# Encoder layer on one core: the Fourier branch on sums and differences of mirrored tokens, channels and weight rows, with three gate blocks ahead of the attention

## The chip, the cores and the metric

The kernel runs on one core of one Trainium2 chip. The metric is the device time of one execution in microseconds (us). Five engines work beside each other, each through its own queue of instructions: PE (TensorE) multiplies matrices, and its weight loads are shown apart as PEld; DVE (VectorE) and ACT (ScalarE) do elementwise work; POOL (GpSimd) does a little; SP (SyncE) starts the transfers from HBM. Instructions wait for each other through semaphores.

## The reference

One layer of a bidirectional encoder on 256 tokens of 2048 channels, in float32:

```python
def _macaron_ffn(x, pre_g, w_gate, w_up, w_down, post_g):
    return x + MACARON_WEIGHT * _rms_norm(_swiglu(_rms_norm(x, pre_g), w_gate, w_up, w_down), post_g)
...
def _fourier_mix(f):
    b, s = f.shape[0], f.shape[1]
    fg = f.astype(jnp.float32).reshape(b, s, FOURIER_GROUPS, FOURIER_GROUP_DIM)
    mixed = jnp.real(jnp.fft.fft2(fg, axes=(1, 3), norm='ortho'))
    return mixed.reshape(b, s, FOURIER_WIDTH).astype(f.dtype)
...
    u = _rms_norm(h, pre_g)
    q, k, v, f, g = jnp.split(u @ w_in, SPLIT_POINTS, axis=-1)
    q = _apply_axial_rope(_rms_norm(q.reshape(b, s, N_Q_HEADS, HEAD_DIM), q_norm_g), rope)
    k = _apply_axial_rope(_rms_norm(k.reshape(b, s, N_KV_HEADS, HEAD_DIM), k_norm_g), rope)
    v = v.reshape(b, s, N_KV_HEADS, HEAD_DIM)
    y_attn = _blocked_gqa(q, k, v) @ w_attn_o
    y_four = _fourier_mix(f) @ w_fourier
    gates = jax.nn.sigmoid((g.reshape(b, s, N_BRANCHES, D_MODEL) + b_gate).astype(jnp.float32)).astype(h.dtype)
    merged = gates[:, :, 0] * y_attn + gates[:, :, 1] * y_four
    return h + _rms_norm(merged @ w_out, post_g)
```

The layer is a first feed-forward half-step (width 5632), the gated mixers above, and a second feed-forward half-step. `w_in` has 2048 columns of q, 512 of k, 512 of v, 1024 of f (8 groups of 128 channels) and twice 2048 of gates; there are 16 query heads on 4 key heads.

## The kernel before

**Products.** Every float32 product is made of three matmuls in the fp32r format (`mm3`, L97 to L100): both factors are split into a rounded part (`hi`) and what is left (`lo`), and hi*hi, hi*lo and lo*hi are summed in PSUM. `split` (L92 to L95) does this with one copy on ACT (L93) and one subtraction on DVE (L94). A weight piece is two k-tiles of 128 x 512; `piece` loads it into a buffer `raw` (five of them) and splits it into `whi` and `wlo` (six pairs). So DVE and ACT can be at most six pieces ahead of PE.

**Blocks.** `col_block` (L179) multiplies the normalised tokens `u` (two token tiles of 128) with 512 columns of a weight: 16 k-tiles, two token tiles, three matmuls each, 96 matmuls of 512 columns. `between` spreads other work over such a block. `row_block` (L209) multiplies a chunk of 512 channels with 512 rows of a weight, again 96 matmuls, and DVE adds the result to `y`.

**The mixers' order.** v (with the norms of the first half-step's end), q of the first four heads, the two blocks of f (L556); then four rounds j, one for each key head: the gate block of the Fourier branch (`gate(12 + j)`, with the Fourier transforms in the first of them), the scores of four heads (`attn_scores`, L609), the Fourier branch's output columns (`four_cb`, L677), the next q block with the products with v between its matmuls (`attn_parts`), and the attention's output rows. The gates of the attention branch (blocks 8 to 11 of `w_in`) come in and after the last round, with `merged` (L711) and the rows of `w_out` between them.

**The Fourier branch.** f is computed for 256 tokens and 1024 channels with 192 matmuls of 512 columns (`fch`). For each group of 128 channels `fourier_positions` (L566) multiplies with the cosines and sines of the positions (six matmuls of 258 columns), and `fourier_channels` (L578) with those of the channels (six matmuls of 130 and 128 columns); the sines of position 256 - k are those of k negated, so only positions 0 to 128 are computed. `four_cb` multiplies the result with `w_fo`: 192 matmuls of 512 columns over the four rounds.

**Scores.** `attn_scores` makes four score tiles `sc` of two heads each, in a ring of three PSUM tiles. For each, DVE takes the maximum (`mx`, L619) and negates it (`nmx`), ACT takes the exponential of both halves (L624), and DVE forms `rinv` and scales `p` (L629). The fourth tile needs the room of the first. ACT loads a table of functions before the gate's sigmoid (L673) and another before the exponential.

**What sets the order.** The code is written in one order, and a scheduler puts the instructions of each engine into one fixed sequence when the kernel is built. On the chip each engine goes through its sequence in that order: an instruction that waits holds up everything behind it on its engine.

Of the kernel before, what the change touches and what calls it, by code (L numbers as in the profile page):

```python
# [18 lines left out]
P = 128  # L19
D = 2048  # L20
# [10 lines left out]
GROUPS = 8  # L31
EPS = 1e-6
# [14 lines left out]
def encoder_layer(  # L47
# [4 lines left out]
    mix_pre, w_in, b_gate, q_g, k_g, w_ao, w_fo, w_out, mix_post,  # L52
    f2_pre, f2_gate, f2_up, f2_down, f2_post,
    rope_cos, rope_sin, dft_pos, dft_ch, ident_in,
# [49 lines left out]
    def piece(src, k0, n, pools=None):  # L104
        """k-tiles k0 .. k0 + n of a chunk of weights: raw, hi, lo."""
# [73 lines left out]
    def col_block(u, w, nb, between=()):  # L179
        """u @ w[nb] for both token tiles: PSUM tiles. between: pieces of other work, spread over the block."""  # L180
# [3 lines left out]
        for kg in range(KD // CK):  # L184
            wt = weights(w[nb, kg])
            for k in range(CK):
                kk = kg * CK + k
                if done < len(between) and kk >= (done + 1) * step:
# [8 lines left out]
    def row_part(ch, wt, t, cb, y, first=False, part=slice(0, NB)):  # L197
# [5 lines left out]
        if first:  # L203
            V.tensor_copy(dst, ps)
# [4 lines left out]
    def row_block(ch, w, rb, y, first, between=()):  # L209
        """y += ch @ w[rb]; between[cb] comes ahead of column block cb."""  # L210
# [7 lines left out]

    def last_rows(ch, w, rb, y, norm, nxt=None, w_next=None):
        """The last row block, token tile 0 first, and the norms behind it; then the first column block of what  # L220
        follows, its token tile 0 while token tile 1 gets ready. VectorE's order is given: it has the most to do here."""
# [97 lines left out]
    class PostNorm:  # L319
        """h += half * rms_norm(y) * g_post per token tile."""  # L320
# [40 lines left out]
    class NextInput:  # L361
        """u = transpose(h * g_pre), rs[t] = rsqrt(mean(h^2)); y is room."""
# [32 lines left out]
    def ffn(u, rs, wg, wu, wd, y, tail, gate0, w_next=None, early=()):  # L395
        """tail() loads what the end needs and gives what to do with y."""
# [36 lines left out]
    zero = const.tile([P, NB], BF16, name="zero")  # L433
# [44 lines left out]
    # column blocks of w_in: 0-3 q, 4 k, 5 v, 6-7 f, 8-11 gate A, 12-15 gate B  # L478
# [4 lines left out]
    gq = const.tile([P, HD], F32, name="gq")  # L483
    gk = const.tile([P, HD], F32, name="gk")
    load(gq[:], q_g.partition_broadcast(P))
    load(gk[:], k_g.partition_broadcast(P))
    rc = const.tile([P, NT, HD], F32, name="rc")
    rsn = const.tile([P, NT, HD], F32, name="rsn")
# [14 lines left out]
    def norm_rope(ps, nm, t):  # L503
        """r * ps, RMS norm of each head, gain and rotation."""
# [3 lines left out]
        junk = work("junk")  # L508
        A.activation(q[:], ps[t][:], AF.Copy, scale=rs[t][:, 0:1])
        for j in range(4):  # L510
            A.activation(junk[:, j * HD:(j + 1) * HD], q[:, j * HD:(j + 1) * HD], AF.Square,
                         accum_out=ssq[:, j:j + 1])
        r = rsqrt(ssq[:], 4, 1.0 / HD, "rh")
        q3 = q[:].rearrange("p (j c) -> p j c", j=4)
        V.tensor_tensor(out=q3, in0=q3, in1=r[:].unsqueeze(2).to_broadcast([P, 4, HD]), op=ALU.mult)
# [13 lines left out]
    pv = col_block(u, w_in, 5, between=[nxt.finish])  # L529
    kro = [norm_rope(pk, "k", t) for t in range(NT)]  # L530
    vs = big("vs", F32R, [P, 2, NT, NB])
    for t in range(NT):
# [282 lines left out]
```

## Time and profile before

| | |
|---|---|
| median of 3 runs | 2108.99 us (2108.08 to 2109.59) |
| span of the profiled execution | 2107.7 us |
| ACT busy | 971.3 us (46%) |
| weight splits on DVE (L94, x727) | 887.3 us, 1221 ns each |
| weight splits on ACT (L93, x727) | 769.1 us, 1059 ns each |
| chain that ended last | PE 96%, DVE 3%, DMA 1% |
| moved by DMA | 406.23 MB, 193 GB/s on average |

The chain that ended last is the work followed back from the last instruction, at each step to what released it. It lies almost all on PE, so in this kernel time is first of all matmul time; the other engines' work counts where PE must wait for it. A matmul's duration in the profile (390 ns for 512 columns) runs until its last result is out, and the next one starts before that; what a matmul costs is the distance between starts.

### The profile page before, as it was taken

How to read it: one execution, taken by the hardware profiler on the slowest of the kernel's cores; microseconds unless marked ns; L12 is line 12 of the kernel's file. 1: busy time of each engine (PE TensorE's matmuls, PEld its weight loads, DVE VectorE, ACT ScalarE, POOL GpSimd, SP SyncE). 2: the span in 40 equal slices, each digit the busy share in tenths (PEclk: the TensorE clock that was granted, in tenths of full speed). 3: DMA queues.
4: the chain of work that ended last, by engine and by line, in shares of the span. 5: the costliest groups of instructions: out<-in, count | busy, mean ns of one | idle time of the engine just before them, and what ended most of it. 6: DMA issues, size and time to landing. Idle time of an engine off the chain costs nothing.

```text
span 2107.7 us, 25198 instructions
## 1 busy us (share of the span) xinstructions
PE 2089.4 (99%) x9528; PEld 1729.8 (82%) x9528; DVE 1290.4 (61%) x1660; ACT 971.3 (46%) x1232; POOL 33.3 (2%) x30
## 2 busy tenths in 40 slices
PE   9999999999999999999999999999999999999998
PEld 7888888888888878888888888778888888888886
DVE  6655555555555786676767666875555555555556
ACT  7444444444444555555455444554444444444443
POOL 0000000000000100000000000200000000000001
PEclk9999999999999999999999999999999999999999
DMA  8665655665656566455545556556566556665563
GB/s 313 229 216 190 190 191 189 196 189 188 193 191 192 178 216 202 145 195 200 180 156 184 191 194 194 194 196 209 193 189 191 189 192 195 189 190 187 194 192 108
DMA packets 112874, 406.23 MB, mean 193 GB/s; under 512 B 12528, under 2 KB 14320, under 8 KB 111344
## 3 DMA queue, kind: packets, MB, share of 16 engines
q1 hardware_dynamic: 112752, 404.61, 59.1%
q8 instruction: 75, 1.23, 0.2%
q14 instruction: 47, 0.39, 0.1%
HBM read 400.37 MB, written 4.19 MB: 192 GB/s over the span
## 4 chain that ended last, share of the span: by engine, by line
PE 96%; DVE 3%; DMA 1%; issue 0%; ACT 0%; SPq 0%; DVEq 0%; ACTq 0%
PE pc L100 20%; PE pc L99 20%; PE pc L98 20%; PE pr L98 10%; PE pr L100 10%; PE pr L99 10%; PE pt L169 2%; PE pf L98 1%; PE pf L100 1%; PE pf L99 1%; DVE wlo L94 1%; DVE h L356 0%; PE pt L640 0%; DMA raw<-in_f_gate 0%; DVE y L206 0%
## 5 line engine op out<-in xcount | busy, mean ns | idle before, releaser
L94 DVE TENSOR_TENSOR wlo<-raw,whi 128x1024 fp32r<-128x1024 f32 (+1 forms) x727 | 887.3, 1221 | 741.9 <-ACT whi L93 741.6
L93 ACT ACTIVATE whi<-raw 128x1024 fp32r<-128x1024 f32 (+1 forms) x727 | 769.1, 1059 | 1009.7 <-PE pc L100 606.7
L98 PE MATMUL pc<-whi,uh 128*128 128x512 f32 x1904 | 744.2, 391 | 1.8 <-ACT uh L451 1.8
L100 PE MATMUL pc<-whi,ul 128*128 128x512 f32 x1904 | 741.6, 390 | 2.3 <-DVE ul L94 2.3
L99 PE MATMUL pc<-wlo,uh 128*128 128x512 f32 x1904 | 741.6, 390 | 2.2 <-DVE wlo L94 2.2
L100 PEld LDWEIGHTS pc<-whi,ul 128*128 128x128 f32 x1904 | 357.4, 188 | 77.6 <-DVE ul L94 3.2
L99 PEld LDWEIGHTS pc<-wlo,uh 128*128 128x128 f32 x1904 | 357.5, 188 | 76.7 <-DVE wlo L94 4.2
L98 PEld LDWEIGHTS pc<-whi,uh 128*128 128x128 f32 x1904 | 357.5, 188 | 76.0 <-ACT uh L451 3.4
L98 PE MATMUL pr<-whi,hTh 128*128 128x512 f32 x688 | 269.5, 392 | 0.0
L100 PE MATMUL pr<-whi,hTl 128*128 128x512 f32 x688 | 268.0, 389 | 0.0
L99 PE MATMUL pr<-wlo,hTh 128*128 128x512 f32 x688 | 267.7, 389 | 0.0
L100 PEld LDWEIGHTS pr<-whi,hTl 128*128 128x128 f32 x688 | 129.1, 188 | 27.0
L99 PEld LDWEIGHTS pr<-wlo,hTh 128*128 128x128 f32 x688 | 129.2, 188 | 26.2
L98 PEld LDWEIGHTS pr<-whi,hTh 128*128 128x128 f32 x688 | 129.2, 188 | 26.1
L206 DVE TENSOR_TENSOR yf<-pr,yf 128x512 f32<-128x512 f32 (+1 forms) x82 | 55.1, 672 | 10.4 <-PE pr L100 9.7
L206 DVE TENSOR_TENSOR y<-pr,y 128x512 f32<-128x512 f32 x80 | 54.7, 685 | 4.1 <-PE pr L100 3.6
L98 PE MATMUL pr<-whi,oTh 128*128 128x512 f32 x128 | 49.8, 389 | 0.0
L99 PE MATMUL pr<-wlo,oTh 128*128 128x512 f32 x128 | 49.8, 389 | 0.0
L100 PE MATMUL pr<-whi,oTl 128*128 128x512 f32 x128 | 49.8, 389 | 0.0
L98 PE MATMUL pr<-whi,mTh 128*128 128x512 f32 x120 | 46.9, 391 | 0.0
L100 PE MATMUL pr<-whi,mTl 128*128 128x512 f32 x120 | 46.7, 389 | 0.0
L99 PE MATMUL pr<-wlo,mTh 128*128 128x512 f32 x120 | 46.7, 389 | 0.0
(218 smaller groups left out, 1188.2 us busy)
## 6 DMA issues: line engine op xcount, KB each, us to landing
raw<-in_f_up SPq DMA_DIRECT2D x176, 512.0 KB, 4.7
raw<-in_f_down SPq DMA_DIRECT2D x176, 512.0 KB, 4.6
raw<-in_f_gate SPq DMA_DIRECT2D x175, 512.0 KB, 4.6
raw<-in_w_in SPq DMA_DIRECT2D x128, 512.0 KB, 4.4
raw<-in_w_ao SPq DMA_DIRECT2D x32, 512.0 KB, 3.9
raw<-in_w_out SPq DMA_DIRECT2D x32, 512.0 KB, 4.5
raw<-in_w_fo SPq DMA_DIRECT2D x16, 512.0 KB, 4.7
h<-in_x SPq DMA_DIRECT2D x2, 1024.0 KB, 8.6
```

The source lines that it names most:

```text
L93: a = A.activation(hi, src, AF.Copy)
L94: v = V.tensor_tensor(out=lo, in0=src, in1=hi.bitcast(F32), op=ALU.subtract)
L98: T.matmul(ps, lh, rh, start=first, stop=False)
L99: T.matmul(ps, lh, rl, start=False, stop=False)
L100: return T.matmul(ps, ll, rh, start=False, stop=last)
L169: T.transpose(pt[:, j, :], src[:, j * P:(j + 1) * P], ident[:])
L206: V.tensor_tensor(out=dst, in0=ps, in1=dst, op=ALU.add)
```

## The change

Mirrored items (position p and 256 - p, channel c and 128 - c, and the rows of `w_fourier` likewise) have equal cosines and opposite sines, so the transform can run on sums and differences, each half as large.

- **Token order.** On the host the tokens are put in mirrored order (`_mirror`), so that token tile 1 is the mirror of tile 0, and the result is put back. `fold_tokens` makes sum and difference of the two tiles of the normalised tokens on DVE and transposes them (`ueo`): 32 transposes in all, in the v block and the first gate block.
- **f.** `fold_f` takes a piece of f's weight (16 pieces), makes sums and differences of mirrored channels on DVE (`dif`, and in place in `raw`), splits both, and multiplies the 260 sum columns with the token sums and the 252 difference columns with the token differences: 12 matmuls a piece, 192 in all. The tokens 0 and 128, which are no mirrored pair, are put right with a running sum `zs` on DVE, two steps a piece. The pieces are woven into the first q block (5), gate block 11 (6) and gate block 12 (5) by the new argument `at` of `col_block`.
- **Transforms.** `fourier_positions` and `fourier_channels` have 42 and 44 small matmuls, of 126 to 130 columns, in place of 48 of 258 and 48 of 128 to 130.
- **Output.** `fourier_out(cb)` takes the place of `four_cb`: for each of four pieces of `w_fo` DVE makes the sum `s` and the difference (in place in `raw`) of mirrored weight rows, both are split, and 6 matmuls follow; channel 64 of each group and token 128 are added by three further matmuls (`mids`, and `first` with `dh` and `dl`, the split of a running sum `acc` kept on DVE). That is 27 matmuls of 512 columns in each round, in place of 48. Sum and difference of the two PSUM tiles then give the two token tiles (`w`), and these are multiplied with the gates.
- **Order.** The gates of the Fourier branch (blocks 10 to 13) now come ahead of the rounds and are kept in `mB`; the attention's gates take their place in the rounds. The merge and the rows of `w_out` follow the last round without gate blocks between them; the first two row blocks of `w_out` are summed in PSUM (`row_blocks`).
- **Moved from DVE to ACT.** The scaling of `p`, the scaling in `norm_rope`, and the first copy of each row result.

```diff
+    def fold_f(b, k0):
...
+        dif = work("dif", [P, WP, OW])
+        V.tensor_tensor(out=dif[:].rearrange("p k (g c) -> p k g c", g=GH), in0=pc, in1=qc, op=ALU.subtract)
+        V.tensor_tensor(out=pc, in0=pc, in1=qc, op=ALU.add)
...
+        split(hi[:, :, 0:EW], lo[:, :, 0:EW], raw[:, :, 0:EW])
+        split(hi[:, :, EW:NB], lo[:, :, EW:NB], dif[:])
+        for j in range(WP):
...
+            mm = mm3(pfold[b][:, e], ueo[0][0][:, k, :], ueo[0][1][:, k, :], hi[:, j, e], lo[:, j, e], k == 0, False)
+            with tc.issue_after(mm.ins):
+                mm3(pfold[b][:, o], ueo[1][0][:, k, :], ueo[1][1][:, k, :], hi[:, j, o], lo[:, j, o], False, k == KD - 1)
...
+                V.scalar_tensor_tensor(out=zs[b], in0=raw[:, j, 0:EW], scalar=o0[:, k:k + 1], in1=zs[b],
+                                       op0=ALU.mult, op1=ALU.add)
...
-                V.tensor_scalar(out=p[:, i, :], in0=p[:, i, :], scalar1=rinv[:, i:i + 1], scalar2=None, op0=ALU.mult)
+                A.activation(p[:, i, :], p[:, i, :], AF.Copy, scale=rinv[:, i:i + 1])
...
-    def four_cb(cb, gz):
+    def fourier_out(cb):
...
+        for j in range(4):
...
+            V.tensor_tensor(out=s[:], in0=raw[:, 0, :], in1=raw[:, 1, :], op=ALU.add)
+            V.tensor_tensor(out=raw[:, 1, :], in0=raw[:, 0, :], in1=raw[:, 1, :], op=ALU.subtract)
...
+            split(hi[:, 0, :], lo[:, 0, :], s[:])
+            split(hi[:, 1, :], lo[:, 1, :], raw[:, 1, :])
+            mm3(pe[:], foT[0][0][:, j, P:2 * P], foT[0][1][:, j, P:2 * P], hi[:, 0, :], lo[:, 0, :], j == 0, False)
+            mm3(po[:], foT[0][0][:, j, 0:P], foT[0][1][:, j, 0:P], hi[:, 1, :], lo[:, 1, :], j == 0, False)
...
+                V.scalar_tensor_tensor(out=acc[:], in0=s[:], scalar=dcol[:, j:j + 1], in1=acc[:], op0=ALU.mult, op1=ALU.add)
...
+        T.matmul(pe[:], mids[:], wn[0:NYR, :], start=False, stop=True)
+        dh, dl = workr("dh"), workr("dl")
+        split(dh[:], dl[:], acc[:])
+        T.matmul(po[:], first[:], dh[:], start=False, stop=False)
+        T.matmul(po[:], first[:], dl[:], start=False, stop=True)
...
+        for t, op in ((0, ALU.add), (1, ALU.subtract)):
+            w = work("w")
+            V.tensor_tensor(out=w[:], in0=pe[:], in1=os_[:], op=op)
+            V.tensor_tensor(out=cbs(mB[t], cb), in0=w[:], in1=cbs(mB[t], cb), op=ALU.mult)
+    gate(10, mB, 0, between=[lambda b=b: fold_tokens(b) for b in range(1, 4)]
+         + [lambda t=t: kro.append(norm_rope(pk, "k", t)) for t in range(NT)])
+    pq = col_block(u, w_in, 0, at=folds_at(5))
+    qs = []
+    gate(11, mB, 1, at=folds_at(6), between=[lambda t=t: qs.append(norm_rope(pq, "q", t)) for t in range(NT)])
+    gate(12, mB, 2, at=folds_at(5), between=[lambda t=t: turn_k(t) for t in range(NT)])
+    qT = new_chunk("qT")
+    gate(13, mB, 3, between=fourier_parts() + [lambda t=t: turn_q(qT, qs, t) for t in range(NT)])
...
     for j in range(4):
...
+            gate(5 + j, zA, j - 1, between=[lambda t=t: turn_q(qT, qs, t) for t in range(NT)])
         for t in range(NT):
             attn_scores(j, qT, t, ps)
-        four_cb(j, gz)
+        fourier_out(j)
```

Where the instructions now stand is shown at two places.

**The scores of a round, on DVE.** Before, in the first round, from the second gate tile on (`z` is the gate, `wlo` a split of weights for `four_cb` and the block behind it):

```order
L672 SCALAR_TENSOR_TENSOR z<-pc,r1r,bg 128x512
L619 TENSOR_REDUCE mx<-sc 128x2
L94 TENSOR_TENSOR wlo<-raw,whi 128x1024
L620 TENSOR_SCALAR nmx<-mx 128x2
L627 RECIPROCAL rinv<-rsum 128x2
L619 TENSOR_REDUCE mx<-sc 128x2
L629 TENSOR_SCALAR p<-p,rinv 128x256 x2
L620 TENSOR_SCALAR nmx<-mx 128x2
L94 TENSOR_TENSOR wlo<-raw,whi 128x1024
```

The same place in the change, from the third `rinv` of the first round on (`s` and `raw` are sum and difference of the first piece of `w_fo`):

```order
L732 RECIPROCAL rinv<-rsum 128x2
L724 TENSOR_REDUCE mx<-sc 128x2
L725 TENSOR_SCALAR nmx<-mx 128x2
L790 TENSOR_TENSOR s<-raw 128x512
L732 RECIPROCAL rinv<-rsum 128x2
L785 TENSOR_TENSOR wn<-nraw,wn 8x512
L791 TENSOR_TENSOR raw<-raw 128x512
L100 TENSOR_TENSOR wlo<-s,whi 128x512
L799 TENSOR_SCALAR acc<-s,dcol 128x512
L100 TENSOR_TENSOR wlo<-raw,whi 128x512
```

Before, the weights that PE needs behind the scores are split before the scores or between them; now the first of `w_fo` is touched behind the fourth maximum, and its split behind the fourth `rinv`. This is so in all four rounds.

**The same place on PE.** Before, the fourth score tile stands 17 matmuls of `four_cb` (`pf`) behind the third; these are the rows from the end of the third tile on, and the fourth begins at the next `sc` row:

```order
L100 MATMUL sc<-kT,qTl 128x256
L98 MATMUL pf<-whi,foTh 128x512
L99 MATMUL pf<-wlo,foTh 128x512
L100 MATMUL pf<-whi,foTl 128x512
L98 MATMUL pf<-whi,foTh 128x512
L99 MATMUL pf<-wlo,foTh 128x512
```

In the change the four score tiles stand together, and these rows, which begin with the last piece of `w_fo`, are the end of `fourier_out` (`pc` is the next q block):

```order
L104 MATMUL pf<-whi,foTh 128x512
L104 MATMUL pc<-whi,uh_5545 128x512
L104 MATMUL pc<-whi,uh_5695 128x512
L105 MATMUL pf<-wlo,foTh 128x512
L106 MATMUL pf<-whi,foTl 128x512
L104 MATMUL pf<-whi,foTh 128x512
L804 MATMUL pf<-wn,mids 128x512
L105 MATMUL pf<-wlo,foTh 128x512
L106 MATMUL pf<-whi,foTl 128x512
L807 MATMUL pf<-dh,first 128x512
L105 MATMUL pc<-wlo,uh_5545 128x512
```

Of the next block five matmuls stand ahead of the last one of `fourier_out` (`first` with `dl`), and all others behind it.

**The folds, on DVE.** A fold of f in the first q block of the change, which no row of before answers to (`wlo<-raw,whi 128x1024` is a whole weight piece of the block):

```order
L615 TENSOR_TENSOR dif<-raw 128x504
L630 SCALAR_TENSOR_TENSOR zs<-raw,o_5824,zs 128x260
L616 TENSOR_TENSOR raw<-raw 128x2x4x63
L100 TENSOR_TENSOR wlo<-dif,whi 128x2x252
L630 SCALAR_TENSOR_TENSOR zs<-raw,o_5824,zs 128x260
L100 TENSOR_TENSOR wlo<-raw,whi 128x2x260
L630 SCALAR_TENSOR_TENSOR zs<-raw,o_5824,zs 128x260
L100 TENSOR_TENSOR wlo<-raw,whi 128x1024 x2
```

A piece of f had one row of 128x1024 on DVE before; a fold has six.

More of the change, by code (lines that the diff above doesn't have):

```diff
@@ L592, in fourier_parts, with constant @@
-    def fourier_parts():
-        held = []
-        def part(n):
-            if n < 8:
-                new = fourier_positions(*divmod(n, 4))
-            if n > 0:
-                fourier_channels(*divmod(n - 1, 4), held.pop())
-            if n < 8:
-                held.append(new)
-        return [lambda n=n: part(n) for n in range(9)]
+    def constant(src, n):
+        raw = work("draw", [P, n])
+        load(raw[:], src)
+        return raw
+    WE, WO = P + 2, P
+    dps = const.tile([P, 2, WE + WO], F32R, name="dps")
@@ new lines, in _constants @@
+    odd = np.zeros((P, P + 2))
+    odd[:, 1:P:2] = 1.0
+    first = np.zeros((P, P))
+    first[:, 0] = 1.0
+    sign = 1.0 - 2.0 * (c % 2)
+    alt = np.zeros((P, GROUPS // 2, NYR))
+    mid = np.zeros((GH, 2 * P + 2 * NYR))
+    for g in range(GROUPS):
+        for at in (0, 32, 64):
+            alt[(g % 2) * HW:(g % 2 + 1) * HW, g // 2, at + g] = sign
+            mid[g % GH, 2 * P + (g // GH) * NYR + at + g] = 1.0
+        if g < GH:
+            mid[g, g * HW:(g + 1) * HW] = sign
+    ones = np.concatenate([odd, first, alt.reshape(P, -1)], 1)
```

354 lines of the change are left out of this document (236 added, 118 removed).

## The prediction

> **What bounds the kernel now.** I read the page's first part, then what PE waited for, then one round of the attention in a table of stretches, then the timeline of its scores.
>
> ```profile
> span 2107.7 us, 25198 instructions
> PE 2089.4 (99%) x9528; PEld 1729.8 (82%) x9528; DVE 1290.4 (61%) x1660; ACT 971.3 (46%) x1232; POOL 33.3 (2%) x30
> ```
> ```profile
> PE pc L100 <- DVE ul L94: 2.3, 2, 1.2
> PE pc L99 <- DVE wlo L94: 2.2, 3, 1.0
> ```
> ```profile
> core 0: us, PE busy (x) PEld busy (x) DVE busy (x) ACT busy (x) POOL busy (x), PEclk, DMA share, GB/s
> 887.80:972.80 85.00, 85.00 (x409) 71.06 (x408) 58.70 (x99) 45.00 (x74) 0.00 (x0) 1.00 0.59 201
> ```
>
> PE is busy for 99% of the span; its largest wait group is 2.3 us. In a round (from its first score matmul to the next round's) PE is busy for all 85 us, at full clock (1.00), and DVE for 58.7. So every matmul taken away shortens the time, as long as PE stays fed; DVE has 26.3 us to spare in a round, though not at every place. The question is where the change spends them.
>
> **The matmuls: 38.5 us less.**
>
> ```profile
> 499.65 0.39 PE L99 MATMUL pr<-wlo,hTh 128*128 128x512 f32 x1
> ...
> 505.77 0.39 PE L99 MATMUL pr<-wlo,hTh 128*128 128x512 f32 x1
> ```
> ```profile
> 856.36 0.28 PE L98 MATMUL pa<-dps,fh 128*128 128x258 f32 x1
> ...
> 857.08 0.40 PE L98 MATMUL pc<-whi,uh 128*128 128x512 f32 x1
> ```
> ```profile
> 862.19 0.22 PE L98 MATMUL pb<-ah,dcs 128*128 128x130 f32 x1
> ...
> 862.81 0.45 PE L98 MATMUL pc<-whi,uh 128*128 128x512 f32 x1
> ```
> ```profile
> 905.88 0.60 PE L640 MATMUL pt<-ident,p 128*128 128x128 f32 x4
> 906.24 0.48 PE L98 MATMUL pc<-whi,uh 128*128 128x512 f32 x1
> ```
>
> Starts give the cost: 27 steps from 499.65 to 505.77 are 0.227 us for 512 columns; six of 258 columns take 0.72 (0.12 each); six of 130 and 128 take 0.62 (0.103 each: these no longer shrink with their columns); four transposes 0.36. Removed: 384 of 512 columns (f and `four_cb`) 87.1, eight times 0.72 and eight times 0.62, together 97.8 us. Added: 192 of 252 or 260 columns at 0.12, 23.0; 86 small ones at 0.103, 8.9; eight fours of transposes, 2.9; 108 of 512, 24.5; together 59.3. The difference is **38.5 us**. Small ones with few stationary columns are not in the trace; between nothing and 0.103 for some twenty of them this is at most 2 us.
>
> **What DVE must do more.**
>
> ```profile
> L94 DVE TENSOR_TENSOR wlo<-raw,whi 128x1024 fp32r<-128x1024 f32 x725 | 885.9, 1223 | 737.5 <-ACT whi L93 737.2
> L94 DVE TENSOR_TENSOR wlo<-raw,whi 128x512 fp32r<-128x512 f32 x2 | 1.4, 692 | 4.4 <-ACT whi L93 4.4
> L525 DVE TENSOR_TENSOR o<-o,tmp 128x512 f32<-128x512 f32 x10 | 6.8, 682 | 0.1
> L356 DVE SCALAR_TENSOR_TENSOR h<-yo,cr,h 128x512 f32<-128x512 f32 x8 | 6.3, 795 | 0.0
> L356 DVE SCALAR_TENSOR_TENSOR h<-yf,cr,h 128x256 f32<-128x256 f32 x4 | 1.7, 477 | 0.0
> L629 DVE TENSOR_SCALAR p<-p,rinv 128x256 f32<-128x256 f32 x32 | 9.7, 345 | 0.0
> ```
>
> A sum, a difference or a half split of 512 columns is 0.68 or 0.69, a step of `acc` 0.80, a step of `zs` 0.48. Two instructions that don't need each other overlap by about 0.08 (the gates `z` in the timeline below start 0.66 apart and take 0.74).
>
> **The rounds: 66 us of new waiting.** This is the term that decides.
>
> ```profile
> 972.52 0.74 DVE L672 SCALAR_TENSOR_TENSOR z<-pc,r0r,bg 128x512 f32<-128x512 f32 x1
> 972.80 0.28 PE L98 MATMUL sc<-kT,qTh 128*128 128x256 f32 x1
> ...
> 973.18 0.74 DVE L672 SCALAR_TENSOR_TENSOR z<-pc,r1r,bg 128x512 f32<-128x512 f32 x1
> ...
> 975.38 1.16 ACT L673 ACTIVATE z<-z 128x512 f32<-128x512 f32 x2
> ...
> 976.54 1.28 ACT L624 ACT_TABLE_LOAD   x1
> 977.84 0.48 ACT L624 ACTIVATE p<-sc,nmx 128x256 f32<-128x256 f32 x1
> ...
> 978.65 0.20 ACT L624 ACTIVATION_READ_ACCUMULATOR p<-sc,nmx 128x1 f32 x1
> 978.89 0.17 DVE L627 RECIPROCAL rinv<-rsum 128x2 f32<-128x2 f32 x1 [3.16 <-ACT p L624]
> 978.91 0.39 PE L98 MATMUL sc<-kT,qTh 128*128 128x256 f32 x1
> ...
> 982.44 0.16 DVE L627 RECIPROCAL rinv<-rsum 128x2 f32<-128x2 f32 x1
> 982.51 0.67 DVE L619 TENSOR_REDUCE mx<-sc 128x2 f32<-128x512 f32 x1
> ...
> 983.62 0.16 DVE L620 TENSOR_SCALAR nmx<-mx 128x2 f32<-128x2 f32 x1
> ...
> 984.87 0.17 DVE L627 RECIPROCAL rinv<-rsum 128x2 f32<-128x2 f32 x1
> ```
>
> The fourth score tile starts only when ACT is done with the first (978.91, 6.1 us behind the first matmul). Before, PE fills that gap and the rest of the softmax with `four_cb`, whose weights were split in time. In the change there is nothing to fill it: each split of `w_fo` stands behind the fourth `mx` or later on DVE (the order shown above), and on PE `fourier_out` stands behind all four score tiles.
>
> I count from the first score matmul. `z` ends at 1.1; the two sigmoids 0.58 each end at 1.75 (the sigmoid's table is loaded earlier now); the exponential's table 1.28, two exponentials 1.0: the first `rinv` stands at 4.1. Each further tile costs `rinv` 0.17, `mx` 0.67, `nmx` 0.16 and 1.0 on ACT, 2.1 with the gaps (2.43 from 982.44 to 984.87, with the scaling of `p` between, which goes to ACT). The third `rinv` is at 8.3, the fourth at 10.4, and `wn` waits for an ACT copy of 0.6: DVE is free for the weights at 11.0. From there to `dl` stand one `wn`, three `s`, four `raw`, eight half splits, five steps of `acc` (one of them a scaling, some 0.6), a whole split (1.22) and `dl`: 16.7 us by rows, 15.3 with 17 overlaps. PE goes past the last matmul of `fourier_out` at **26.3 us**. Until then it has 24 score matmuls (0.12 each, 2.9) and 31 of 512 columns (7.0). It stands for **16.4 us** a round, 66 in four. Behind it the next block's splits take 1.22 against 2.72 us of matmuls a piece, so nothing further is late.
>
> Bounds: two instructions on 8 partitions (`wn`, the last `acc`) may cost 0.16 (the row of two columns, `rinv`) instead of 0.7, and more may overlap: 13 a round. With a tenth more for semaphores on the 26.3 us: 19.
>
> **The folds: 7 us.** From the end of gate block 10 (DVE's `z` waits for it, so it starts there without a lead) to the last fold's split, DVE has 16 folds of 3.7 (two of 0.68, 1.38 of splits, two `zs` of 0.48; 3.46 with overlaps), less the last two `zs`, 54.4; 22 whole pieces at 1.14, 25.1; two `norm_rope` of 3.7, 7.4; `z` twice 1.3; `fl` and `kT` 0.6 each: 90.8. PE has the q block and gate block 11 (21.8 each), 13 of 16 k-tiles of block 12 (17.7), 15 folds of 1.44 and two fours of transposes (0.7): 83.6. The difference is **7 us**; 0 if all neighbours overlap, 15 if none do and every fold waits 0.1 for ACT.
>
> **The rest: nothing.** The three gate blocks only change places. The merge is covered by the last rows of `w_ao` (on DVE eight pieces 9.8, eight row sums and eight merge steps 5.5 each, four splits 2.8, together 23.6 us, against 96 matmuls and 16 transposes, 23.2, on PE, with six pieces ahead). First copies and the scaling of `p` go to ACT, which has 40 of 85 us free; if that cover were gone they would cost 0.69 each. Constants are loaded in the v block.
>
> **The sum.** 2107.7 - 38.5 + 66 + 7 = 2142.2 for the span; the median of the runs is 1.3 us above the span: **2144 us**, 1.7% slower.
>
> **The rivals.**
>
> *PE stays fed.* If DVE did the sums of `w_fo` in its gaps (it stands idle 3.16 us before the first `rinv` above) and the folds had a lead, the 38.5 us would stay: 2107.7 - 38.5 + 1.3 = **2070**. For it speaks the 26.3 us of spare DVE time in a round; against it the fixed order, which does not let DVE reach `s` before the fourth `mx`. The point that decides: with a wait under 38.5 / 4 = 9.6 us a round, folds free, the kernel is not slower. With both terms at their lower bounds it still is (52 against 38.5). Chance 0.08; 0.04 for ending between, within 0.2% of 2109.
>
> *The clock falls.* PE stands from about 4.9 (four score tiles) to 11.6, almost 7 us.
>
> ```profile
> 1.22 3.44 PE L437 MATMUL idle<-zero 128*128 128x512 bf16 x8 [1.22 <-DVE zero L434]
> ```
>
> At the program's start, after idling, eight matmuls of 512 columns take 3.44 us, 0.43 each instead of 0.227. If PE is slow again after each long wait, the paced part hides it (31 at 0.43 are 13.3 of 15.3 us), but eight matmuls behind it cost 0.2 more each, 1.6 us a round, or twice that if it takes two such stretches: 6.5 to 13 us in all, **2150 to 2157**. The Trainium skill ("TensorE: Matmul & The Clock Gate", Part 1) says that the array falls to half its clock after at least one idle window of about 3.4 us and comes back after a busy one. By that rule each round would pay; before, no wait inside the program is long enough to show it. Chance 0.25.
>
> *The folds cost more.* If ACT and DVE wait on each other at every fold, 15 to 25 us: **2152 to 2162**. Within the forecast's range.
>
> **How the numbers follow.** Slower as reckoned 0.63, with the clock's loss 0.25, fed 0.08, between 0.04. The lowest sum with waits is 2107.7 - 38.5 + 52 + 0 + 1.3 = 2122, the highest 2107.7 - 38.5 + 76 + 15 + 13 + 1.3 = 2175; some room at both ends gives 2118 to 2178. Faster by over 0.2% 0.08, within 0.2% 0.04 (about what a measurement of this kernel can tell from no change), slower 0.88.
>
> **What would show it.** In the profile of the changed kernel PE's idle time stands before `pf` (released by DVE `wlo`) and before the fourth `sc`, in four equal places; DVE is near 100% there from the fourth `rinv` to `dl`; a round's PE busy time falls by 4.8 us ((48 - 27) matmuls) while the round grows by some 12. In the blocks with folds PE waits for `wlo` before `pe`, a few us in all. PEclk below 1.0 behind the waits would show the second rival. The prediction is wrong if PE is busy all through the rounds, or if it waits there for DMA.

## The result, and the profile after

| | before | after |
|---|---|---|
| median | 2109.29 us (2108.08 to 2110.31, 4 runs) | 2155.06 us (2151.13 to 2158.72, 4 runs) |
| ratio to before | | 1.0218, 95% interval 1.0203 to 1.0232 |
| span of the profiled execution | 2107.7 us | 2152.7 us |
| matmuls | 9528 | 9466 |

The change makes the kernel 2.2% slower; 2144 us was forecast, with a range of 2118 to 2178. First the page of the changed kernel (busy times, two rows of its 40 slices, the chain that ended last):

```profile
span 2152.7 us, 25270 instructions
...
PE 2081.0 (97%) x9466; PEld 1711.2 (79%) x9466; DVE 1333.1 (62%) x1746; ACT 1017.9 (47%) x1369; POOL 33.4 (2%) x30
...
DVE  6545555555555878948586677685455555555556
...
PEclk9999999999999999989898989999999999999999
...
PE 87%; DVE 9%; ACT 2%; DMA 1%; issue 1%; SPq 0%; DVEq 0%; ACTq 0%
```

There are fewer matmuls and PE is busy less, in a longer span; the chain lies on PE for 87% in place of 96%, and on DVE for 9% in place of 3%. From the 14th to the 27th slice (some 700 to 1450 us) DVE's digits rise to 8 and 9, and the granted clock falls at four places, the rounds. What PE waited for (us in all, times, longest us):

```profile
PE pf L104 <- ACT whi L99: 26.9, 8, 6.4
PE sc L104 <- ACT p L729: 8.2, 4, 2.4
PE pe L105 <- DVE wlo L100: 6.5, 7, 1.6
PE pf L105 <- DVE wlo L100: 5.8, 13, 0.7
PE pe L104 <- ACT whi L99: 3.3, 6, 1.1
```

`pf` and `sc` are the rounds (`fourier_out` and the fourth score tile), `pe` the folds. The long waits before `pf` end with ACT's `whi`, not with DVE's `wlo`, which the prediction had named as their sign. These waits are shorter than what is lost, because a matmul's duration runs until its last result is out. So I took the starts: the distance from each matmul to the next, less what it costs when PE is fed (0.227 us for 512 columns, 0.1205 for about 256, 0.103 for about 130, 0.09 for a transpose), summed over a stage. This is the loss by waits and by slow starts together:

| loss in us | before | after | w_fo in the gate block (first experiment) |
|---|---|---|---|
| start, first half-step, up to the first fold | 11.6 | 10.7 | 10.3 |
| blocks with folds | - | 16.8 | 17.3 |
| block with the transforms | 1.5 | 5.7 | 3.5 |
| four rounds | 2.8 | 67.8 | 4.0 |
| rest | 8.2 | 5.9 | 5.8 |
| sum | 24.2 | 106.8 | 40.8 |
| span less the sum: fed matmuls, and some 11 us ahead of the first and behind the last | 2083.5 | 2045.9 | 2046.7 |

The difference of 45.0 us in the span is therefore 37.6 us fewer of matmuls and 82.6 us more of loss: 65.0 in the rounds, 16.8 in the folds, 4.1 in the transforms' block, and 3.3 less elsewhere. The last two columns have the same matmuls, so a value of this count is good to about 0.8 us.

A round, and the blocks with folds, in a table of stretches:

```profile
core 0: us, PE busy (x) PEld busy (x) DVE busy (x) ACT busy (x) POOL busy (x), PEclk, DMA share, GB/s
1051.16:1147.46 96.30, 85.69 (x388) 68.74 (x387) 66.72 (x112) 51.55 (x95) 0.00 (x0) 0.93 0.48 157
816.90:914.10 97.20, 87.33 (x451) 71.55 (x450) 89.03 (x153) 49.47 (x85) 0.00 (x0) 0.98 0.63 207
```

The round of 85.0 us takes 96.3. PE's busy time in it did not fall by the 4.8 us that the prediction gave as a sign (85.7 against 85.0), because the durations of matmuls at half clock or behind a wait are longer. DVE is busy for 66.7 of it, so the round has room for DVE's work; the third round's timeline of PE shows where it is missing (start, duration, idle time before and its releaser):

```profile
1147.46 0.28 PE L104 MATMUL sc<-kT,qTh 128*128 128x256 f32 x1
...
1151.72 0.39 PE L104 MATMUL sc<-kT,qTh 128*128 128x256 f32 x1 [1.94 <-ACT p L729]
...
1159.07 0.80 PE L104 MATMUL pf<-whi,foTh 128*128 128x512 f32 x1 [6.29 <-ACT whi L99]
1160.58 0.80 PE L105 MATMUL pf<-wlo,foTh 128*128 128x512 f32 x1 [0.72 <-DVE wlo L100]
1161.17 0.63 PE L106 MATMUL pf<-whi,foTl 128*128 128x512 f32 x1
1161.60 0.63 PE L104 MATMUL pf<-whi,foTh 128*128 128x512 f32 x1
...
1173.51 0.40 PE L808 MATMUL pf<-dl,first 128*128 128x512 f32 x1
```

and DVE beside it:

```profile
1156.77 0.69 DVE L790 TENSOR_TENSOR s<-raw 128x512 f32<-128x512 f32 x1
1158.01 0.17 DVE L732 RECIPROCAL rinv<-rsum 128x2 f32<-128x2 f32 x1 [0.56 <-ACT p L729]
1158.52 0.68 DVE L785 TENSOR_TENSOR wn<-nraw,wn 8x512 fp32r<-8x512 f32 x1 [0.35 <-ACT wn L784]
...
1172.58 0.67 DVE L100 TENSOR_TENSOR dl<-acc,dh 128x512 fp32r<-128x512 f32 x1
```

Counted from 1147.46: the fourth `rinv` stands at 10.55 (10.4 forecast), `wn` at 11.1 (11.0), `dl` ends at 25.8, and PE's last matmul of `fourier_out` starts at 26.05 (26.3). The four rounds give 26.5, 26.05, 26.05 and 26.05. From `wn` to `dl` DVE has no gap over 0.04 us; PE stands for 6.3 us, until ACT is done with the exponentials, the copy of `wn` and the first `whi`, and then follows DVE. The first `s` waits for the fourth `nmx` although `w_fo` does not depend on the scores.

### The profile page after: what moved, and what is told of

Same layout as the page of the kernel before. It is cut to its first block, busy times and chain, and to the rows that moved or that the text cites. A ratio compares the mean times of both kernels' runs of the same rounds, so it can differ in the third digit from the quotient of the medians.

```text
span 2152.7 us, 25270 instructions
## 1 busy us (share of the span) xinstructions
PE 2081.0 (97%) x9466; PEld 1711.2 (79%) x9466; DVE 1333.1 (62%) x1746; ACT 1017.9 (47%) x1369; POOL 33.4 (2%) x30
## 3 DMA queue, kind: packets, MB, share of 16 engines
q8 instruction: 74, 1.21, 0.2%
## 4 chain that ended last, share of the span: by engine, by line
PE 87%; DVE 9%; ACT 2%; DMA 1%; issue 1%; SPq 0%; DVEq 0%; ACTq 0%
PE pc L105 18%; PE pc L106 18%; PE pc L104 18%; PE pr L105 10%; PE pr L104 10%; PE pr L106 10%; DVE wlo L100 3%; PE pt L175 1%; ACT p L729 1%; DMA raw<-in_w_f 1%; DVE raw L791 0%; DVE h L385 0%; DVE zs L630 0%; ACT p L734 0%; DVE dif L615 0%
## 5 line engine op out<-in xcount | busy, mean ns | idle before, releaser
L100 DVE TENSOR_TENSOR wlo<-raw,whi 128x1024 fp32r<-128x1024 f32 (+2 forms) x727 | 867.8, 1198 | 675.3 <-ACT whi L99 673.5
L99 ACT ACTIVATE whi<-raw 128x1024 fp32r<-128x1024 f32 (+2 forms) x727 | 752.9, 1040 | 892.6 <-PE pc L106 508.6
L104 PE MATMUL pc<-whi,uh 128*128 128x512 f32 x1840 | 720.2, 392 | 3.2 <-ACT whi L99 1.8
L105 PE MATMUL pc<-wlo,uh 128*128 128x512 f32 x1840 | 718.2, 390 | 2.9 <-DVE wlo L100 2.9
L106 PE MATMUL pc<-whi,ul 128*128 128x512 f32 x1840 | 717.6, 390 | 1.9 <-DVE ul L100 1.9
L105 PEld LDWEIGHTS pc<-wlo,uh 128*128 128x128 f32 x1840 | 346.1, 188 | 76.2 <-DVE wlo L100 6.3
L104 PEld LDWEIGHTS pc<-whi,uh 128*128 128x128 f32 x1840 | 345.9, 188 | 75.4 <-ACT whi L99 3.0
L106 PEld LDWEIGHTS pc<-whi,ul 128*128 128x128 f32 x1840 | 346.0, 188 | 74.8 <-DVE ul L100 2.8
L217 DVE TENSOR_TENSOR yf<-pr,yf 128x512 f32<-128x512 f32 (+1 forms) x82 | 55.1, 673 | 10.4 <-PE pr L106 9.7
```

The source lines that it names most:

```text
L99: a = A.activation(hi, src, AF.Copy)
L100: v = V.tensor_tensor(out=lo, in0=src, in1=hi.bitcast(F32), op=ALU.subtract)
L104: T.matmul(ps, lh, rh, start=first, stop=False)
L105: T.matmul(ps, lh, rl, start=False, stop=False)
L106: return T.matmul(ps, ll, rh, start=False, stop=last)
L217: V.tensor_tensor(out=dst, in0=ps, in1=dst, op=ALU.add)
```

## The experiments

The runs were compared with the kernel before on the same chip; its median lay between 2108.1 and 2108.5 us. "The round" is a round of the attention.

| run | median, us | ratio to before, 95% |
|---|---|---|
| w_fo in the gate block | 2090.05 | 0.9912 (0.9897 to 0.9926) |
| without most of `acc` | 2143.99 | 1.0171 (1.0156 to 1.0186) |
| gap filled with matmuls | 2153.87 | 1.0217 (1.0201 to 1.0232) |
| without most of `zs` | 2148.65 | 1.0191 (1.0174 to 1.0208) |
| w_fo in the gate block, and: folds one ahead | 2094.79 | 0.9932 (0.9919 to 0.9946) |
| folds two ahead | 2098.93 | 0.9954 (0.9942 to 0.9967) |
| one ahead, `dif` on POOL | 2098.51 | 0.9952 (0.9939 to 0.9964) |
| four buffers `raw` | 2102.35 | 0.9975 (0.9965 to 0.9986) |
| six working tiles | 2090.08 | 0.9915 (0.9901 to 0.9928) |
| six buffers `raw`, six working tiles | 2086.94 | 0.9898 (0.9883 to 0.9913) |
| the same, folds 6, 4, 6 | 2089.24 | 0.9910 (0.9897 to 0.9924) |

**The weights of `w_fo` prepared in the gate block.** `fourier_prep` holds the loads, `s`, `raw`, the splits, `acc` and `wn` of `fourier_out`, one part for each piece of `w_fo`; `fourier_out` keeps the matmuls, `dh` and `dl` (`wn` uses the room of the cosines of positions, which are done with by then).

```diff
-    gate(13, mB, 3, between=fourier_parts() + [lambda t=t: turn_q(qT, qs, t) for t in range(NT)])
+    prep, *four = fourier_prep(0)
+    gate(13, mB, 3, between=fourier_parts() + [lambda t=t: turn_q(qT, qs, t) for t in range(NT)] + prep)
...
-            gate(5 + j, zA, j - 1, between=[lambda t=t: turn_q(qT, qs, t) for t in range(NT)])
+            prep, *four = fourier_prep(j)
+            gate(5 + j, zA, j - 1, between=[lambda t=t: turn_q(qT, qs, t) for t in range(NT)] + prep)
...
-        fourier_out(j)
+        fourier_out(j, *four)
```

> The loads, sums, differences and splits of w_fo and the running sum acc of each round stand in the gate block ahead of its scores (piece by piece, by the block's argument between); the matmuls of fourier_out stay behind the scores. My theory: in the changed kernel PE stands some 17 us a round (67 us by the starts of its matmuls) because these DVE steps come behind the fourth maximum; done earlier they lie beside a gate block's matmuls, where DVE has room, and 15 to 17 us a round go: 2155 - 60 to 67 = 2088 to 2095, with PE passing the last matmul of fourier_out some 10 to 12 us behind the first score matmul instead of 26. Rival one, the softmax itself is what PE waits for (the fourth exponential ends about 9 us behind the first score matmul, against 5 us of PE work): at most the part behind it goes, about 6.5 us a round, 2129. Rival two, DVE has too much work over the whole round: the wait moves into the gate block, and the time stays above 2140.

Measured: 2090.05 us, 65.0 below the changed kernel and 0.9% below the one before. Its second round in the table of stretches, and PE's timeline from the first score matmul:

```profile
1033.47:1113.79 80.32, 80.32 (x389) 67.01 (x387) 66.47 (x112) 50.22 (x95) 0.00 (x0) 1.00 0.57 187
```
```profile
1033.47 0.28 PE L104 MATMUL sc<-kT,qTh 128*128 128x256 f32 x1
...
1035.62 0.40 PE L104 MATMUL pf<-whi,foTh 128*128 128x512 f32 x1
...
1039.27 0.39 PE L105 MATMUL pf<-wlo,foTh 128*128 128x512 f32 x1
1039.57 0.39 PE L104 MATMUL sc<-kT,qTh 128*128 128x256 f32 x1
...
1048.87 0.41 PE L822 MATMUL pf<-dl,first 128*128 128x512 f32 x1
```

DVE has the same work in a round (66.5 against 66.7 us), yet the round takes 80.3 us with PE busy throughout: 16.0 less than in the changed kernel, and 4.7 less than before, which is the 21 matmuls that it has fewer. The 17 `pf` matmuls from 1035.62 to 1039.27 fill the time up to the fourth score tile, as `four_cb` did. The last matmul of `fourier_out` stands at 15.4 us, not at the 10 to 12 I expected, because matmuls of the next block stand ahead of it in PE's order; nothing is lost there. Both rivals fall: the last exponential ends 13.9 us behind the first score matmul, later than the 10.4 of the changed kernel, and PE is busy all the same; and DVE's total fits.

**Less DVE work in the stretch that PE follows.** The four later steps of `acc` in each round are left out.

```diff
-            else:
-                V.scalar_tensor_tensor(out=acc[:], in0=s[:], scalar=dcol[:, j:j + 1], in1=acc[:], op0=ALU.mult, op1=ALU.add)
-        g = slice(0, GROUPS)
-        V.scalar_tensor_tensor(out=acc[g, :], in0=nraw[g, :], scalar=dcol[g, 4:5], in1=acc[g, :], op0=ALU.mult, op1=ALU.add)
```

> Left out: the four later steps of the running sum acc in each round (its first step, the split into dh and dl and all matmuls stay), so the value of token 128's share is wrong in the output. It takes four DVE instructions away from the stretch in which PE waits, 0.66 us each from start to start, 2.6 us. My theory (PE's end of fourier_out is set by DVE's instructions one behind the other): 2.6 us a round less, 10.6 in all, 2144.5. Rival, the wait is for the softmax chain or for the transfers of w_fo: under 2 us in all, 2153 to 2155.

Measured: 2143.99 us, 11.1 less. The second round in the table of stretches:

```profile
1050.78:1144.89 94.11, 84.27 (x389) 68.78 (x387) 64.00 (x108) 51.45 (x95) 0.00 (x0) 0.93 0.48 161
```

The last matmul of `fourier_out` comes at 24.0 us in place of 26.05 and the round takes 94.1 us in place of 96.3. So 2.0 to 2.2 of the 2.6 us taken from DVE in this stretch are kernel time.

**The gap filled, to keep the clock up.**

```diff
+        with tc.issue_after(mm.ins):
+            for _ in range(54):
+                T.matmul(pe[:, 0:WE + WO], first[:], dps[:, 0, :], start=True, stop=True)
```

`mm` is the last score matmul of the round.

> 54 matmuls of 258 columns on constants (0.12 us each, 6.5 us) are put between the fourth score tile and the first matmul of fourier_out in each round; what they write is overwritten. They fill the one long wait of 6.4 us, behind which the 512-column matmuls of the changed kernel start 0.43 us apart instead of 0.227 for some 4 us. My theory: the slow stretch is hidden, since DVE paces PE there anyway: no change within 2 us, 2153 to 2157, with starts 0.227 us apart behind the first piece and the last matmul of fourier_out still 26 us behind the first score matmul. Rival (the second rival of the prediction), the slow stretch costs time of its own: 1.6 us a round or twice that, 2142 to 2149.

Measured: 2153.87 us, no difference from the changed kernel. PE's timeline in its second round, which begins at 1048.88:

```profile
1054.44 7.66 PE L784 MATMUL pf<-dps,first 128*128 128x258 f32 x54
1061.93 0.40 PE L104 MATMUL pf<-whi,foTh 128*128 128x512 f32 x1
1062.17 0.39 PE L105 MATMUL pf<-wlo,foTh 128*128 128x512 f32 x1
...
1068.47 0.63 PE L106 MATMUL pf<-whi,foTl 128*128 128x512 f32 x1
1068.90 0.63 PE L104 MATMUL pf<-whi,foTh 128*128 128x512 f32 x1
...
1074.92 0.40 PE L812 MATMUL pf<-dl,first 128*128 128x512 f32 x1
```

Behind the fill the starts are 0.24 us apart instead of 0.43, so the clock was up; the last matmul still stands at 26.04 us behind the first score matmul (26.04 to 27.4 in the four rounds). The cleanest of them is the third, in which the clock never falls:

```profile
1145.04:1241.21 96.17, 89.69 (x440) 72.77 (x439) 66.18 (x111) 51.43 (x95) 0.00 (x0) 1.00 0.48 156
```

It takes 96.2 us and its last matmul stands at 26.05, as in the changed kernel. So the slow stretch is real, but it lies inside the time that DVE sets. It is not free everywhere: in the first and the fourth round of this run the clock falls for 3.4 us some 23 us into the round (974.82 and 1264.95), at the end of that stretch, and the last matmul comes 0.9 us later than in the same rounds of the changed kernel.

**Less DVE work in the folds.** All steps of `zs` but the first of each half are left out.

```diff
-            else:
-                V.scalar_tensor_tensor(out=zs[b], in0=raw[:, j, 0:EW], scalar=o0[:, k:k + 1], in1=zs[b],
-                                       op0=ALU.mult, op1=ALU.add)
```

> Left out: all steps but the first of the running sum zs (two STT of 260 columns a fold), so tokens 0 and 128 have a wrong share in f. It takes 30 DVE instructions of 0.40 us (start to start) away, 12 us, and lets a fold's buffer raw go as soon as it is split. My theory: in the blocks with folds DVE has more to do than PE, and PE waits there 16.7 us by the starts of its matmuls (7 was forecast): with 12 us of DVE work less, 10 to 14 us go, 2141 to 2145. Rival, the wait is the path through one fold (difference, copy on ACT, subtraction) at each fold, whatever DVE has to do: 0 to 4 us go, 2151 to 2155.

Measured: 2148.65 us, 6.4 less, between both. The loss in the folds falls from 16.8 to 13.5, that in the transforms' block from 5.7 to 2.9. The second of these falls can't be credited to the edit: in the run with the filled gap, whose instructions are the same as the changed kernel's up to there, that block loses about 3 us too, so it differs that much from execution to execution. The blocks with folds, and what DVE waited for around them:

```profile
817.10:910.90 93.80, 86.82 (x450) 72.50 (x449) 78.43 (x124) 50.44 (x86) 0.00 (x0) 0.96 0.65 219
```
```profile
DVE dif L615 <- DMA raw<-in_w_f: 6.5, 4, 3.2
DVE wlo L100 <- ACT whi L99: 3.3, 6, 1.5
```

PE's fed matmuls there are 93.8 - 13.5 = 80.3 us, and DVE's work is now 78.4: DVE has less to do than PE, and PE still loses 13.5. A comparison of totals doesn't explain the folds. DVE now stands for 93.8 - 78.4 = 15.4 us there, against 97.2 - 89.0 = 8.2 in the changed kernel.

**A lead for the folds.** On top of the first experiment each fold's loads, sums, splits and `zs` are written one fold (or two) ahead of its matmuls, the first in gate block 10; in a third version `dif` is also made on POOL.

```diff
+    def fold_step(a):
+        fold_f(*a)
+        if ahead:
+            fold_prep(*ahead.pop(0))
...
-        V.tensor_tensor(out=dif[:].rearrange("p k (g c) -> p k g c", g=GH), in0=pc, in1=qc, op=ALU.subtract)
+        nc.gpsimd.tensor_tensor(out=dif[:].rearrange("p k (g c) -> p k g c", g=GH), in0=pc, in1=qc, op=ALU.subtract)
```

> Built on the run with w_fo prepared in the gate block (2090). Each fold's load, sums, splits and steps of zs are written one fold ahead of its matmuls, the first of them in gate block 10. My theory: part of the 17 us that PE loses in the blocks with folds is a missing lead: at the first two folds alone 3.9 us go (0.9, 1.3 and 1.8 by the starts), because DVE begins them behind the gate's z, and a part of the later waits of 0.5 to 1.5 us before pe goes too; DVE is rid of one fold (3.5 us) of the 89 us that it is busy there, and the blocks' PE work is 80 us. So 17 falls to 9 to 13, and the time to 2082 to 2086. Rival, DVE's total alone sets the wait and a lead buys nothing but the first fold's work: 13.5 to 17 stay, 2087 to 2090.

> The same with two folds ahead, the first two in gate block 10. My theory (lead and DVE's total together): 3.5 us of DVE's work more go out of the blocks, 6 to 10 us of loss stay, 2079 to 2083. Rival: two folds that wait for their matmuls take two of the six split buffers from the blocks' own pieces, which come late instead: no better than one fold ahead, or 1 to 4 us worse.

> One fold ahead, and the difference dif of each fold on POOL instead of DVE. It takes 16 instructions of 0.68 us, some 10 us, from DVE in these blocks; POOL, idle there, takes about 1.4 us each (its products of 512 columns in the profile take that). My theory (DVE's total): 4 to 8 us less than with the lead alone, 2075 to 2081. Rival: DVE is slower while POOL works: in the changed kernel DVE's products y<-h,gpre take 1.19 us each (2.38 for two at 733.41) with POOL at work beside them, and 0.69 without; 16 such stretches would give back 8 us or more, so no gain, or 1 to 4 us worse than the lead alone.

Measured: 2094.79, 2098.93 and 2098.51 us, that is 5 to 9 us worse than without a lead; none of these expectations of a gain held. What their rivals said of two folds ahead and of POOL (no better than the lead alone, or 1 to 4 us worse) held, nearly: 4.1 and 3.7 us worse. For one fold ahead the rival's 2087 to 2090 is missed too. In that run, what PE and DVE waited for around these blocks:

```profile
PE pc L106 <- DVE wlo L101: 11.5, 8, 3.0
```
```profile
DVE dif L616 <- DMA raw<-in_w_f: 10.3, 5, 3.2
```

The waits before `pe` are all but gone; in their place PE waits for the blocks' own pieces (`pc`), and DVE for transfers of `w_f`. In gate block 10 and before, the loss rises from 4.9 to 11.8 us between 600 us and the first fold's matmul, and in the folds 16.7 remain. With `dif` on POOL, the rows of these blocks beside those of the kernel with the lead alone, whose first two rows come first:

```profile
L101 DVE TENSOR_TENSOR wlo<-raw,whi 128x1024 fp32r<-128x1024 f32 x25 | 29.9, 1220 | 2.9 <-ACT whi L100 2.9
L617 DVE TENSOR_TENSOR raw<-raw 128x504 f32<-128x504 f32 x15 | 10.2, 679 | 0.2
```
```profile
L101 DVE TENSOR_TENSOR wlo<-raw,whi 128x1024 fp32r<-128x1024 f32 x25 | 32.6, 1326 | 2.0 <-ACT whi L100 2.0
L616 POOL TENSOR_TENSOR dif<-raw 128x504 f32<-128x504 f32 x14 | 21.6, 1546 | 76.4 <-DMA raw<-in_w_f 54.7 <-issue 6.5 <-DVE wlo L101 4.8
L617 DVE TENSOR_TENSOR raw<-raw 128x504 f32<-128x504 f32 x15 | 11.1, 742 | 14.7 <-POOL dif L616 14.7
```

DVE's sum in place has to wait for POOL's difference (14.7 us), and the means of DVE's own instructions rise by 9% (1220 to 1326 ns, 679 to 742): three of the 25 splits take 1.96 to 2.20 us and one of the 15 sums 1.65, all others as long as before. The ten us taken from DVE come back as a wait.

**The buffers that a fold holds.** On top of the first experiment, the number of buffers `raw` is changed. The six-buffer version needs room and has six working tiles instead of eight; the control has the six tiles alone.

```diff
-RAW_BUFS = 5
+RAW_BUFS = 6
...
-    wk = pool("wk", 8)
+    wk = pool("wk", 6)
```

> Built on the run with w_fo prepared in the gate block (2090). Six buffers raw for weights as they are loaded instead of five; for their room the pool of working tiles has six instead of eight. In the blocks with folds SP's queue waits 45 us in all for steps of zs, which hold a fold's raw, and DVE stands 3 to 4 us for raw of w_f. My theory: the folds cost more than reckoned because these buffers are held, so one more gives 2 to 5 us: 2085 to 2088 (if the two working tiles are not missed; the run with six working tiles and five buffers shows that). Rival, DVE's own work and its order set the wait: within 1.5 us of that control run.

> The control: five buffers raw, six working tiles instead of eight. Either theory: between 2090 (the tiles are not missed) and some 2100 (they are); its distance to the run with six buffers is what a buffer gives.

> The other direction: four buffers raw, eight working tiles. My theory (the buffers held by folds): in the blocks with folds the loss rises from 17 us by 4 to 10, and the time to 2094 to 2100, while the rounds and the feed-forward steps stay as they are. Rival (DVE's own work and order): no change within 2 us there; 2088 to 2092.

Measured: 2086.94 us with six buffers (2085.22 to 2088.17), 2090.08 for the control (2089.53 to 2090.73), 2102.35 with four. What DVE waited for around the folds with four buffers, then with six:

```profile
DVE dif L615 <- DMA raw<-in_w_f: 8.2, 5, 4.5
```
```profile
DVE dif L615 <- DMA raw<-in_w_f: 2.3, 2, 1.3
```

The loss in the folds is 21.2 us with four, 18.0 in the control and 16.2 with six. So the number of buffers is a part of it, a small one: 3.9 us more with four than with five (17.3 in the first experiment), 1.8 less with six than in the control. With four buffers some 10 us more are lost outside the folds (4.6 in the transforms' block, about 4 up to the first fold, the rest behind the rounds), where I had expected no change, and the time misses the 2094 to 2100 that I gave. A sixth buffer is worth some 3 us by the medians; the times of the two versions don't overlap, but the intervals of their ratios do, so its size is not certain.

**The folds spread otherwise.**

```diff
-    pq = col_block(u, w_in, 0, at=folds_at(5))
+    pq = col_block(u, w_in, 0, at=folds_at(6))
...
-    gate(11, mB, 1, at=folds_at(6), between=[lambda t=t: qs.append(norm_rope(pq, "q", t)) for t in range(NT)])
-    gate(12, mB, 2, at=folds_at(5), between=[lambda t=t: turn_k(t) for t in range(NT)])
+    gate(11, mB, 1, at=folds_at(4), between=[lambda t=t: qs.append(norm_rope(pq, "q", t)) for t in range(NT)])
+    gate(12, mB, 2, at=folds_at(6), between=[lambda t=t: turn_k(t) for t in range(NT)])
```

> Built on the run with six buffers raw and w_fo prepared in the gate block (2087). The sixteen folds stand 6, 4 and 6 in the first q block, gate block 11 and gate block 12 instead of 5, 6 and 5. Gate block 11 also has the two norm_rope of q: by the rows DVE has there 9.1 + 7.4 + 1.3 + 20.8 = 38.6 us of work against 30.4 of PE, the q block some 27.7 against 29, block 12 some 28.4 against 29; with 6, 4, 6 DVE has 31 to 32 us in each, against 30.4, 27.6 and 30.4. One theory (the loss is DVE's total over the three blocks, carried along by the six-piece lead, and its standstill for raw): no change, 2085 to 2089. The other (the overfull gate block 11 is what PE waits for): 3 to 6 us less, 2081 to 2084.

Measured: 2089.24 us, no gain: 2.3 us more by the medians, and the intervals of its ratio and of the run that it is built on overlap. Gate block 11 with its two `norm_rope` is not the place that sets the loss.

## Why the prediction was right, and where it was not

**Direction and main term: right, and shown.** "The rounds: 66 us of new waiting" is 65.0 by the starts (67.8 less the 2.8 of before). The steps under it held too, but for the sign of the long wait (ACT's `whi` ends it): the fourth `rinv`, `wn`, `dl` and the end of `fourier_out` stand within 0.3 us of the forecast in the round shown, and the end of `fourier_out` in all four. That the place of `w_fo`'s preparation is the cause is shown from two sides: moved ahead of the scores, the wait goes (4.0 us are left in four rounds); shortened by four instructions of 0.66 us, it shrinks by 2.0 to 2.2 us.

**The matmuls: right.** 38.5 us forecast, 37.6 by the fed starts.

**The folds: the wrong size.** The step that failed is "the difference is 7 us", which took DVE as working without a pause. The rival "the folds cost more" had 15 to 25 us and 2152 to 2162 and so holds the loss of 16.8 and the time; its condition, ACT and DVE waiting on each other at every fold, is not what the waits below show, where DVE waits for ACT once. The sums themselves were near: DVE is busy for 89.0 us (90.8 forecast) and PE's fed matmuls take 97.2 - 16.8 = 80.4 (83.6). But DVE stands for 97.2 - 89.0 = 8.2 us in these blocks. What it waited for in the changed kernel, and then what SP's queue of loads waited for, in the changed kernel (two lines) and without most of `zs` (the third):

```profile
DVE dif L615 <- DMA raw<-in_w_f: 4.1, 3, 1.9
DVE wlo L100 <- ACT whi L99: 1.5, 1, 1.5
DVE z L774 <- PE pc L106: 1.0, 1, 1.0
```
```profile
SPq L80 <- DVE wlo L100: 46.0, 27, 5.1
SPq L80 <- DVE zs L630: 45.1, 11, 16.5
SPq L80 <- DVE wlo L100: 90.0, 40, 16.0
```

8.6 us of DVE's surplus and 8.2 of standstill make the 16.8; that is a division of the measured time and not yet a cause. A fold's `raw` can't be loaded again until its two steps of `zs` are done, so it lies near to blame the buffer that they hold. The run without them speaks against that: the queue then waits 90.0 us for `wlo`, as much as for both before, and DVE stands 6.5 us for `raw` in place of 4.1. Nor does less work on DVE bring much: 10.6 us less of it in these blocks took 3.3 us from their loss, a sixth buffer 1.8. A lead, a shift of work to POOL and another spread gave nothing in the time. So the step that failed is known (DVE does not work without a pause), and why it pauses, in its order, ACT's or the transfers, stays open for most of the loss.

**The transforms' block: left out.** The prediction had "the rest: nothing"; this block loses 4.1 us more than its counterpart before. PE waits 1.2 us for the split of `zs` and then runs at half clock (granted 0.50 from 923.77 to 927.18). About half of it comes and goes: without most of `zs` 2.9 are left, but about 3 also in the run with the filled gap, where the wait is 0.3 us and the clock stays up. The profiled span is 10.5 us over the forecast's 2142.2: 9.8 from the folds, 4.1 from this block and 0.9 from the matmuls, less 1.0 in the rounds and 3.3 elsewhere. The last of these the prediction did not have and no run explains.

**The clock: the mechanism came, the price didn't.** The rival "the clock falls" had 2150 to 2157 and holds the measured time, but for another reason; that is luck. The half clock is there, in the starts 0.43 us apart from 1161.17 on and in the granted clock (0.50 in the third number from the end):

```profile
1152.46:1166.11 13.65, 6.30 (x14) 3.86 (x14) 10.33 (x22) 9.62 (x26) 0.00 (x0) 0.50 0.11 38
```

It fell at 1152.46, behind the wait of 1.94 us for the fourth score tile and some 0.3 us before the wait of 6.3 us began. The Trainium skill ("TensorE: Matmul & The Clock Gate", Part 1) has it fall after at least one idle window of about 3.4 us; here it fell after less. The filled gap shows that it costs nothing in the rounds of the changed kernel, because the paced part hides it, and the eight matmuls behind it that I charged with 0.2 us each start 0.23 apart: the clock is back from 1166.11. The clock also fell for 3.4 us at 869.15, in the folds. Whether slow starts there cost time of their own was not tried.

**PE stays fed: wrong for this order, right as a mechanism.** It was given 0.08 and 2070, against the fixed order; with another order it happens: 2087 to 2090. What is missing to 2070 is the loss in the folds and the transforms.

## What to carry to other kernels

Fewer matmuls only pay if what replaced them is ready when PE gets there: preparation that depends on nothing nearby belongs into a block where the preparing engine has room, not behind the wait that the old matmuls used to cover. A comparison of two engines' totals does not give the wait where each also waits for the other, for loads and for a third engine, in a fixed order: in the folds PE still lost 13.5 us when DVE had less to do than PE. Before charging a fallen clock to the total, see whether another engine paces that stretch, and whether the slow part ends before it does.

## What the runs showed of the hardware that was not expected

PE's clock also halves without a long wait. In the second round of the run with the filled gap it did so twice:

```profile
1053.32:1056.73 3.41, 3.41 (x17) 3.41 (x17) 1.64 (x5) 3.18 (x10) 0.00 (x0) 0.50 0.01 2
1066.98:1070.39 3.41, 3.18 (x7) 1.34 (x5) 3.38 (x7) 1.30 (x3) 0.00 (x0) 0.50 0.58 168
```

The first stretch follows the wait of 1.95 us for the fourth score tile, so the fill itself starts at half clock. Before the second the starts were 0.24 us apart at 1062, and no wait was longer than 0.64 us; PE had worked in short pieces behind DVE for some five us. Three of the four rounds of this run have such a second fall and one has none, so what decides it is not shown. The Trainium skill has a case of frequent short pauses with an oscillating clock in "TensorE: Matmul & The Clock Gate" ("A second HAM failure mode: psum-queue depth-cycling"); the trace here agrees with that, and the rule of one idle window of about 3.4 us (Part 1) would not give it.

A DVE instruction on 8 partitions is not cheaper than on 128: `wn` on 8x512 takes 0.68 us in the rows above, as 128x512 does. The lower bound that the prediction took for it (0.16) was too low.

When POOL and DVE work on SBUF beside each other, the one that starts second can be held up until the other is done. In the run with `dif` on POOL, three of the 25 splits take 1.96 to 2.20 us in place of 1.22, and all three start while a difference runs on POOL: the split of 868.53 beside the difference of 868.22 to 869.41 takes 1.96. Where the split came first it keeps its time and the difference is longer: the split of 909.53 takes 1.21, and the difference of 909.85 takes 1.95 in place of 1.18; in a run of DVE instructions it is POOL that waits as well (2.48 for the difference of 831.69). The mean of 1326 ns a split hides this. The Trainium skill says that the two share their SBUF interfaces, with contention for DVE instructions with two SBUF inputs ("GPSIMD Engine Reference", Specifications), which a split has; this agrees.
